# A layer with 64 experts on one core: another order of the experts, eight early loads on ScalarE's queue, and a last pass written out tile by tile

## The chip, the core and the metric

The kernel runs on one core of a Trainium2 chip. The metric is the device time of one execution in microseconds (us). The core has five engines that each take their instructions in a fixed order: TensorE (PE, matrix products and transposes; PEld is its weight loads), VectorE (DVE), ScalarE (ACT), GpSimd (POOL) and SyncE (SP, which here issues most transfers). Sixteen DMA engines move data between HBM and the core's SBUF. The instructions of one engine never overtake each other; a wait at its head holds all that is queued behind it.

## The reference

One layer for 1024 tokens of width 1024: first token mixers (differential attention beside a state space scan), then a mixture of experts. The change lies in the second half:

```python
h = modulate(rmsnorm(x, g_pre_ffn[li]), sh2, sc2)
f_lat = moe_ffn(h.reshape(-1, d), *moe_w)          # 64 experts, 8 for each token, and one shared
x = x + gt2 * rmsnorm(f_lat.reshape(x.shape), g_post_ffn[li])

def expert_block(args):
    tok_b, w_b, e = args
    xb = h[tok_b]
    hid = jax.nn.silu(xb @ w_e_gate[e]) * (xb @ w_e_up[e])
    return (hid @ w_e_down[e]) * w_b[:, None].astype(h.dtype)
...
routed = jax.ops.segment_sum(out.reshape(n_pad, d), buf_tok, num_segments=n_tok)
return routed + shared
```

Everything is float32. The gate, up and down matrices of one expert are 1 MB each, so 192 MB of weights are read in this half, each matrix once.

## The kernel before

Attention, scan and output projection come first, up to about 1800 us; the change touches none of it. Then tokens are routed, and the shared expert runs on eight tiles of 128 tokens.

**Experts, blocks, places.** Experts are renumbered on the chip by their load, the fullest first, and each number has a fixed room for tokens (CAPS, line 37): 416, 384, 352, 320 for experts 0 to 3, 256 to 128 for 4 to 39, 112 for 40 to 48, 96 for 49 to 56, 80 for 57 to 59 and 64 for 60 to 63. A room is cut into blocks of at most 128 tokens, 98 in all: expert 0 has four, 1 to 3 three, experts up to 28 at least two ("heavy"), 29 to 63 one ("light"). Tokens that find no room would go through a leftover loop (`overflow`, L2330; its count is read from `novf` at L2336 and the loop at L2337 runs that many times, here none).

**Two kinds of blocks.** A block of more than 64 tokens works with weights that were split into a high and a low float32r part (`weights`, `weights_down`: ScalarE casts the high part, L164, VectorE subtracts, L171), with three products for each pair: 24 for gate and up, 12 for down, on 128x512. A block of at most 64 tokens (`whole_block`) reads the raw weights as they were loaded, packed two or four ways on PE; a block of 64 has 64 small gate and up products and 8 down products. Experts 60 to 63 have only such a block ("pure") and are not split. Experts 0, 3 and 13 to 28 have one besides larger blocks, and their raw buffers are given back only when both the split and the block have read them.

**Buffers and queues.** `loads` (L2000) puts three transfers for each expert on SP's queue (helper `dma`, L212): gate, up, down, in the order of the list `order`. There are 4 raw buffers for gate and up, 2 for down (`draw`), 4 high and 4 low tiles for gate and up (`gh`, `gl`), 2 and 2 for down (`dh`, `dl`): two experts' worth of each. Buffers of a ring are handed out in turn. POOL gathers each block's tokens (L262) and adds its result to one of two sums in HBM (`scatter_add`, L268), `yacc[1]` and `yacc[0]` alternately (`turn`, L1995).

**What sets the order.** `Flow` (L107 on) is a planner that runs while the kernel is built: every stage is a generator, and it writes each engine's instructions in the order in which its own clocks would let the stages go on. The list `order` (L2304 and L2305) is what it starts from: one heavy expert, one light one, and so on: 0, 29, 1, 30, 2, 31, 3, 32, and so on to 28, 57, then 58 to 63. I call the position in this list a place: expert 2 is at place 4, 4 at 8, 13 at 26, 20 at 40, 28 at 56 and 63 at 63.

**The last pass** (`final`, L2397): the two sums are loaded as 8 tiles y and 8 tiles z of 128x1024 on SP, in turn y0, z0, y1, z1 and so on, then x for the last two tiles (PLAIN, L31). A group of FG tiles (4, 2, 2) is added (L171), squared on ScalarE with its row sums (L156), a root is computed by 12 small steps on VectorE, and the tiles are scaled (L187). Six tiles are added to the output in HBM by accumulating transfers on POOL (`add_to`, L274), since the output already holds x; for the last two, x is added on VectorE, and a plain write goes out on SP. The planner sets the order of these steps:

```python
for t in range(8):
    for i in range(2):
        F.dma((y, z)[i][t], s.yacc[i][t * P:(t + 1) * P, :])
...
for n in FG:
    F.spawn(1, rows(t, n))
```

## Time and profile before

| what | us |
|---|---|
| median of three runs | 2785.7 (2785.47 to 2786.71) |
| profiled execution | 2800.41 |
| its span, first to last instruction | 2798.6 |
| PE busy | 2618.5 (94%) |
| VectorE busy | 2013.0 (72%) |
| ScalarE busy | 1340.7 (48%) |
| POOL busy | 903.0 (32%) |
| SP's transfers, share of 16 engines | 45.6% |
| POOL's transfers, share of 16 engines | 14.8% |

All times in the sections below are counted from the first instruction of the profiled execution. The mean granted clock of PE is 0.976 of full speed over the span. The chain that ended last, followed back from the last instruction, lies for 58% on PE, 10% on DMA and 9% on VectorE. Busy shares are means over stages of different kinds; the routed experts take from about 1830 to 2740, the last pass the rest.

### The profile page before, as it was taken

The numbers are of one execution on the slowest core, as the hardware profiler recorded it, in microseconds if no ns is written. First come the engines' busy times: TensorE is split into PE (matmuls) and PEld (weight loads), VectorE is DVE, ScalarE is ACT, GpSimd is POOL, SyncE is SP. The second block draws the span as 40 slices with busy tenths as digits, with TensorE's granted clock in tenths as the row PEclk, the third lists the DMA queues.
The fourth block names the chain that finished last, engine by engine and source line by source line (L and its number), as shares of the span: only waits on it lengthen the run. The fifth ranks groups of instructions, "written<-read, shape, count | busy, mean of one in ns | idle before, by whom it ended". The sixth has DMA issues, their size and how long they took to land.

```text
span 2798.6 us, 41131 instructions
## 1 busy us (share of the span) xinstructions
PE 2618.5 (94%) x14561; PEld 2101.1 (75%) x14561; DVE 2013.0 (72%) x4680; ACT 1340.7 (48%) x2104; POOL 903.0 (32%) x669
## 2 busy tenths in 40 slices
PE   7999999999999999999999999889999999999991
PEld 4888878778788777888887687668887776777660
DVE  6877133768686749888894767867788877788863
ACT  4211123344443546666664422435666656676651
POOL 0111010545353520000000000055656656677841
PEclk9999999999999999999999999999999999999996
DMA  7767253242334354223233953568899998999997
GB/s 277 224 206 216 64 143 105 67 139 91 121 91 132 106 172 145 82 91 141 93 102 125 292 179 133 188 216 264 276 309 297 315 299 278 307 321 328 314 316 233
DMA packets 275409, 545.67 MB, mean 195 GB/s; under 512 B 31562, under 2 KB 166835, under 8 KB 248194
## 3 DMA queue, kind: packets, MB, share of 16 engines
q1 hardware_dynamic: 239330, 437.14, 45.6%
q0 software_dynamic: 35872, 105.88, 14.8%
q8 instruction: 115, 1.88, 0.3%
q14 instruction: 92, 0.75, 0.1%
HBM read 433.78 MB, written 124.73 MB: 200 GB/s over the span
## 4 chain that ended last, share of the span: by engine, by line
PE 58%; DMA 10%; DVE 9%; issue 4%; ACT 2%; POOL 2%; SPq 0%; POOLq 0%; ACTq 0%; DVEq 0%
PE gu L148 16%; PE acc L148 10%; PE dn L148 9%; PE bacc L148 5%; PE sps L148 5%; PE pv L148 4%; DMA cr<-cumd,crow 3%; PE xt L152 2%; PE tr L152 2%; PE aux L148 2%; DVE G L187 2%; DMA qk<-qk 2%; DMA braw<-in_w_branch_attn_dram 1%; DVE gl L171 1%; DVE W L180 1%
## 5 line engine op out<-in xcount | busy, mean ns | idle before, releaser
L171 DVE TENSOR_TENSOR gl<-raw,gh 128x1024 fp32r<-128x1024 f32 x240 | 288.2, 1218 | 35.4 <-ACT gh L164 33.7
L148 PE MATMUL acc<-hh,hi 128*128 128x512 f32 (+2 forms) x760 | 304.7, 401 | 1.3 <-DVE ux L187 1.3
L148 PE MATMUL acc<-hl,hi 128*128 128x512 f32 (+2 forms) x760 | 289.3, 381 | 0.0
L164 ACT CAST gh<-raw 128x1024 fp32r<-128x1024 f32 x240 | 246.6, 1050 | 88.0 <-PE gu L148 59.2
L148 PE MATMUL acc<-hh,lo 128*128 128x512 f32 (+1 forms) x736 | 280.9, 382 | 2.5 <-DVE lo L171 2.5
L148 PE MATMUL gu<-gh,xh 128*128 128x512 f32 (+3 forms) x672 | 278.4, 414 | 0.6 <-ACT gh L164 0.6
L148 PE MATMUL gu<-gl,xh 128*128 128x512 f32 (+3 forms) x672 | 264.5, 394 | 6.2 <-DVE gl L171 4.4
L148 PE MATMUL gu<-gh,xl 128*128 128x512 f32 (+3 forms) x672 | 264.5, 394 | 0.0
L193 DVE TENSOR_SCALAR_CACHE_REDUCE e<-sps 128x512 f32<-128x512 f32 (+1 forms) x384 | 214.4, 597 | 32.9 <-PE sps L148 32.6
L262 POOL DMA_INDIRECT cr<-cumd,crow x98 | 123.4, 1260 | 316.1 <-DMA wtab<-sc 281.2
L268 POOL DMA_INDIRECT yacc<-y,tk x98 | 181.3, 1850 | 96.8 <-issue 23.2
L148 PE MATMUL sps<-qk 128*128 128x512 f32 (+1 forms) x768 | 195.6, 386 | 9.3 <-DMA qk<-qk 5.1
L156 ACT ACTIVATE e<-e,st 128x1280 f32<-128x1280 f32 x128 | 174.7, 1366 | 32.0 <-DVE st L202 31.8
L262 POOL DMA_INDIRECT wc<-wtab,tk x98 | 148.6, 1516 | 121.0 <-DVE tk L182 85.9
L148 PE MATMUL acc<-hi,hh 128*128 128x512 f32 x448 | 181.3, 405 | 0.0
L148 PE MATMUL acc<-hi,hl 128*128 128x512 f32 x448 | 176.2, 393 | 0.4 <-DVE hl L171 0.4
L148 PE MATMUL acc<-lo,hh 128*128 128x512 f32 x448 | 176.0, 393 | 0.0
L148 PEld LDWEIGHTS sps<-qk 128*128 128x128 f32 x768 | 141.2, 192 | 41.3 <-DVE e L193 8.3
L148 PEld LDWEIGHTS acc<-hh,hi 128*128 128x128 f32 (+1 forms) x760 | 142.6, 188 | 32.9 <-issue 4.0
L148 PE MATMUL pv<-wr,vv 128*128 128x256 f32 x640 | 165.1, 381 | 0.0
L148 PEld LDWEIGHTS acc<-hl,hi 128*128 128x128 f32 (+1 forms) x760 | 142.6, 188 | 27.4 <-issue 0.8
L148 PEld LDWEIGHTS acc<-hh,lo 128*128 128x128 f32 x736 | 138.7, 188 | 32.1 <-DVE lo L171 3.3
(327 smaller groups left out, 6264.3 us busy)
## 6 DMA issues: line engine op xcount, KB each, us to landing
raw<-in_w_e_gate_dram SPq DMA_DIRECT2D x64, 1024.0 KB
raw<-in_w_e_up_dram SPq DMA_DIRECT2D x64, 1024.0 KB
draw<-in_w_e_down_dram SPq DMA_DIRECT2D x64, 1024.0 KB
qk<-qk POOLq DMA_DIRECT2D x16, 1664.0 KB
raw<-in_w_in_dram SPq DMA_DIRECT2D x40, 512.0 KB
wada<-in_w_ada_dram SPq DMA_DIRECT2D x32, 512.0 KB
R<-acd SPq DMA_DIRECT2D x64, 256.0 KB
qk<-sa SPq DMA_DIRECT2D x52, 256.0 KB
```

The lines of the kernel that those rows point to most:

```text
L148: s.nc.tensor.matmul(out, l, r, start=start, stop=stop)
L152: s.nc.tensor.transpose(out, in_, ident)
L156: s.nc.scalar.activation(out, in_, fn, **kw)
L164: s.nc.scalar.copy(out, in_)
L171: s.nc.vector.tensor_tensor(out, a, b, op=op)
L180: s.nc.vector.tensor_scalar(out, a, s1, s2, op0=op0)
L187: s.nc.vector.scalar_tensor_tensor(out, a, sc, b, op0=op0, op1=op1)
L193: s.nc.vector.tensor_scalar(out, a, s1, None, op0=op0, op1=op1, accum_out=acc)
L262: s.nc.gpsimd.indirect_dma_start(out=out, out_offset=None, in_=table, in_offset=bass.IndirectOffsetOnAxis(ap=idx, axis=0), **kw)
L268: s.nc.gpsimd.indirect_dma_start(out=table, out_offset=bass.IndirectOffsetOnAxis(ap=idx, axis=0), in_=in_, in_offset=None, compute_op=ALU. ...
```

## The change

It has three parts. The list `order` comes from a new function, `balanced`: it prices an expert's work on PE (9.3, 7.2 or 4.4 for a block by its kind) and its load (8.6 + 0.03 for each token of room), and takes an expert with more work than load, then one with less, so that the running difference stays near zero; the last three light ones are kept for the end. The eight z tiles get a pool of their own after the experts and before the leftover loop, and are loaded on ScalarE's queue instead of SP's. The last pass is written in the order of the string TAIL (a: add and square, r: roots of a group, s: scale and write) with groups of 3, 3 and 2 tiles.

```diff
--- before.py
+++ after.py
@@ -28,7 +28,8 @@
 ND, NR, NDR, NA = 2, 4, 2, 5
 LEAD = 2
 SLACK = 400.0, 0.0, 200.0, 0.0, 800.0, 400.0, 1500.0
-FG = 4, 2, 2
+FG = 3, 3, 2
+TAIL = "a0 a1 a2 a3 r0 s0 a4 s1 a5 s2 a6 r1 s3 a7 s4 s5 r2 s6 s7"
 PLAIN = 2
 HELD = 6, 1, 1
 RP = 0
@@ -2301,8 +2302,7 @@
             whole = {r: [] for r in blocks if any(ways(q[2]) > 1 for q in blocks[r])}
             pure = {r for r in whole if len(blocks[r]) == 1}
             uses = {}
-            many, one = [r for r in range(64) if len(blocks[r]) > 1], [r for r in range(64) if len(blocks[r]) == 1]
-            order = [q for i in range(max(len(many), len(one))) for q in many[i:i + 1] + one[i:i + 1]]
+            order = s.balanced(blocks)
             arena = Arena(*(q.get() for q in (gls, ghs, ghs, gls)))
             F.spawn(0, loads())
             F.spawn(2, weights())
@@ -2326,6 +2326,26 @@
             F.spawn(1, routed())
             F.run()
             s.close("em", "ew", "eps")
+            fz = s.open("fz")
+            s.z = [fz.tile([P, D], F32, name=f"z{t}") for t in range(8)]
+            for t in range(8):
+                F.dma(s.z[t], s.yacc[1][t * P:(t + 1) * P, :], eng=nc.scalar)
+
+    def balanced(s, blocks):
+
+        pe = {r: sum({1: 9.3, 2: 7.2, 4: 4.4}[ways(q[2])] for q in b) for r, b in blocks.items()}
+        ld = {r: 8.6 + 0.03 * CAPS[r] for r in blocks}
+        k = sum(pe.values()) / sum(ld.values())
+        last = [r for r in sorted(blocks) if len(blocks[r]) == 1][-3:]
+        left, out, d = [r for r in sorted(blocks) if r not in last], [], 0.0
+        more = {r: pe[r] - k * ld[r] for r in left}
+        while left:
+            same = [q for q in left if (more[q] > 0) == (d <= 0)] or left
+            r = max(same, key=lambda q: abs(more[q]))
+            left.remove(r)
+            out.append(r)
+            d += more[r]
+        return out + last
 
     def overflow(s):
 
@@ -2397,45 +2417,42 @@
     def final(s):
         F = s.F
         with s.pool("fin") as fp:
-            y, z, x1 = ([fp.tile([P, D], F32, name=f"{n}{t}") for t in range(8)] for n in ("y", "z", "x1"))
+            y, x1 = ([fp.tile([P, D], F32, name=f"{n}{t}") for t in range(8)] for n in ("y", "x1"))
+            z = s.z
             for t in range(8):
-                for i in range(2):
-                    F.dma((y, z)[i][t], s.yacc[i][t * P:(t + 1) * P, :])
+                F.dma(y[t], s.yacc[0][t * P:(t + 1) * P, :])
             for t in range(8 - PLAIN, 8):
                 F.dma(x1[t], s.out[0][t * P:(t + 1) * P, :])
             sqs = s.ring(fp, [P, D], "sq", 2)
-
-            def rows(t0, n):
-
-                ss = fp.tile([P, n], F32, name=f"nss{t0}")
-                for i in range(n):
-                    q = y[t0 + i]
-                    yield [q, z[t0 + i], "DVE"]
-                    F.tt(q, q, z[t0 + i], ALU.add)
-                    yield [q, sqs, "ACT"]
-                    sq = sqs.get()
-                    F.act(sq, q, AF.Square, accum_out=ss[:, i:i + 1])
-                    sqs.put(sq)
-                yield [ss, "DVE"]
-                F.ts(ss, ss, 1.0 / D, EPS, ALU.mult, ALU.add)
-                r = yield from s.rsqrt(fp, ss, n, f"z{t0}")
-                for i in range(n):
-                    q, o = y[t0 + i], s.out[0][(t0 + i) * P:(t0 + i + 1) * P, :]
-                    yield [r, "DVE"]
-                    F.stt(q, q, r[:, i:i + 1], s.gpost, ALU.mult, ALU.mult)
-                    if t0 + i >= 8 - PLAIN:
-                        F.tt(q, q, x1[t0 + i], ALU.add)
-                        F.dma(o, q)
-                        continue
-                    yield [q, "POOL"]
+            ss = [fp.tile([P, n], F32, name=f"nss{g}") for g, n in enumerate(FG)]
+            at = [(g, i) for g, n in enumerate(FG) for i in range(n)]
+            root = {}
+
+            def add(t):
+                g, i = at[t]
+                F.tt(y[t], y[t], z[t], ALU.add)
+                sq = sqs.get()
+                F.act(sq, y[t], AF.Square, accum_out=ss[g][:, i:i + 1])
+                sqs.put(sq)
+
+            def roots(g):
+                F.ts(ss[g], ss[g], 1.0 / D, EPS, ALU.mult, ALU.add)
+                root[g] = s.drain(s.rsqrt(fp, ss[g], FG[g], f"z{g}"))
+
+            def scale(t):
+                g, i = at[t]
+                q, o = y[t], s.out[0][t * P:(t + 1) * P, :]
+                F.stt(q, q, root[g][:, i:i + 1], s.gpost, ALU.mult, ALU.mult)
+                if t >= 8 - PLAIN:
+                    F.tt(q, q, x1[t], ALU.add)
+                    F.dma(o, q)
+                else:
                     F.add_to(o, q)
 
-            t = 0
-            for n in FG:
-                F.spawn(1, rows(t, n))
-                t += n
+            for q in TAIL.split():
+                {"a": add, "r": roots, "s": scale}[q[0]](int(q[1]))
             F.run()
-        s.close("rw")
+        s.close("fz", "rw")
 
     def run(s):
         tc, nc, F = s.tc, s.nc, s.F
```

With these prices the list is, with a bar where the pattern changes: 0, 60, 29, 30 | 31, 2, 32, 33, 34, 1, 35, 36, 37, 3, 38, 39, 40, 11, 41, 42, 12, 43, 9, 44, 45, 10, 46, 8, 47, 4, 48, 5, 49, 6, 50, 51, 7, 52 | 13, 53, 14, 54, 15, 55, 56, 16, 57, 17, 58, 18, 59 | 19, 20, 21, 22, 23, 24, 25, 26, 27, 28 | 61, 62, 63. Lines of the changed kernel are one higher than before up to `order`, and 20 higher from `overflow` on.

The order shows on POOL where the first routed blocks are gathered (xg: a block's tokens, wc: their weights, cr: the table from which token numbers are made; tk: token numbers). Before, the blocks behind expert 0's are those of experts 29 and 1, all of 128 tokens:

```order
L262 DMA xg<-htab,tk 128x1024
L262 DMA wc<-wtab,tk 128x1
L262 DMA cr<-cumd,crow 128x128
L262 DMA wc<-wtab,tk 128x1
L262 DMA xg<-htab,tk 128x1024 x2
L262 DMA wc<-wtab,tk 128x1
L268 DMA yacc_13428<-y,tk 4096x256
```

Now the piece at the same place has the block of 64 tokens of expert 60, and the table read of a block of 96:

```order
L263 DMA xg<-htab,tk 64x1024
L263 DMA wc<-wtab,tk 128x1
L263 DMA cr<-cumd,crow 96x128
L263 DMA wc<-wtab,tk 128x1
L263 DMA xg<-htab,tk 128x1024
L269 DMA yacc_13428<-y,tk 4096x256
L263 DMA xg<-htab,tk 128x1024
```

The first scatter, of expert 0's block of 32, stands one step earlier, and a gather of 64 rows has come ahead of it.

On ScalarE at the end of the experts (novf: the count of tokens left over; dn: a block's down result), before:

```order
L156 ACTIVATE y_26499<-dn_26494,wc_25685 128x512
L2336 TENSOR_LOAD novf_16399
L2337 COMPARE_AND_BRANCH
L2337 UNCONDITIONAL_BRANCH x2
L2480 BRANCH_PREFETCH_HINT
```

Now:

```order
L157 ACTIVATE y_26499<-dn_26491,wc_25803 128x512
L213 DMA z0_26510<-yacc1_13428 128x1024
L213 DMA z1_26511<-yacc1_13428 128x1024
L2356 TENSOR_LOAD novf_16303
L2357 COMPARE_AND_BRANCH
```

and behind the loop's end:

```order
L2357 COMPARE_AND_BRANCH
L2357 UNCONDITIONAL_BRANCH
L213 DMA z2_26512<-yacc1_13428 128x1024
L213 DMA z3_26513<-yacc1_13428 128x1024
L213 DMA z4_26514<-yacc1_13428 128x1024
L213 DMA z5_26515<-yacc1_13428 128x1024
L213 DMA z6_26516<-yacc1_13428 128x1024
L213 DMA z7_26517<-yacc1_13428 128x1024
L157 ACTIVATE sq_26736,nss0_26732<-y0_26706 128x1024
```

Two of the eight z loads stand ahead of the leftover loop and six behind its end, ahead of the first square.

On VectorE in the last pass (rs_y: the roots of a group; raw: the gain; nss: sums of squares), before, from the first addition:

```order
L171 TENSOR_TENSOR y0_26687<-y0_26687,z0_26695 128x1024
L171 TENSOR_TENSOR y4_26691<-y4_26691,z4_26699 128x1024
L171 TENSOR_TENSOR y1_26688<-y1_26688,z1_26696 128x1024
L171 TENSOR_TENSOR y5_26692<-y5_26692,z5_26700 128x1024
L171 TENSOR_TENSOR y2_26689<-y2_26689,z2_26697 128x1024
L171 TENSOR_TENSOR y6_26693<-y6_26693,z6_26701 128x1024
L171 TENSOR_TENSOR y3_26690<-y3_26690,z3_26698 128x1024
L182 TENSOR_SCALAR nss4_26730<-nss4_26730 128x2
L171 TENSOR_TENSOR y7_26694<-y7_26694,z7_26702 128x1024
```

Now, behind the first four additions and the roots of group 0:

```order
L188 SCALAR_TENSOR_TENSOR y0_26706<-y0_26706,rs_y_26748,raw_26413 128x1024
L172 TENSOR_TENSOR y4_26710<-y4_26710,z4_26514 128x1024
L188 SCALAR_TENSOR_TENSOR y1_26707<-y1_26707,rs_y_26748,raw_26413 128x1024
L172 TENSOR_TENSOR y5_26711<-y5_26711,z5_26515 128x1024
L188 SCALAR_TENSOR_TENSOR y2_26708<-y2_26708,rs_y_26748,raw_26413 128x1024
L172 TENSOR_TENSOR y6_26712<-y6_26712,z6_26516 128x1024
L183 TENSOR_SCALAR nss1_26733<-nss1_26733 128x3
```

Before, seven additions stand ahead of the first step of a root, and the scalings come after all eight; now scalings of tiles 0 to 2 alternate with additions of tiles 4 to 6.

## Rows read from the trace of the kernel before

**Rows 1.** The page, busy time, share of the span and instructions of each engine.

```profile
PE 2618.5 (94%) x14561; PEld 2101.1 (75%) x14561; DVE 2013.0 (72%) x4680; ACT 1340.7 (48%) x2104; POOL 903.0 (32%) x669
```

**Rows 2.** Windows of the routed stage: length, busy time (count), granted clock, DMA share, GB/s.

```profile
1875.00:2050.00 175.00, 175.00 (x912) 143.62 (x911) 134.75 (x243) 103.34 (x157) 101.65 (x74) 1.00 0.83 256
2050.00:2100.00 50.00, 48.83 (x241) 40.53 (x240) 42.31 (x73) 32.68 (x47) 30.14 (x20) 1.00 0.97 330
2100.00:2275.00 175.00, 172.55 (x896) 135.52 (x895) 148.69 (x261) 111.32 (x167) 112.77 (x76) 0.99 0.95 305
2275.00:2425.00 150.00, 140.47 (x902) 103.79 (x902) 112.48 (x198) 92.76 (x142) 95.78 (x63) 0.98 0.93 293
2425.00:2550.00 125.00, 124.01 (x900) 92.00 (x897) 108.59 (x197) 86.83 (x135) 90.55 (x59) 1.00 1.00 320
2550.00:2725.00 175.00, 163.12 (x1208) 116.15 (x1208) 135.25 (x229) 106.77 (x174) 115.39 (x69) 0.98 0.96 317
```

**Rows 3.** Waits of SP's queue, 1850 to 2735: us in total, times, longest.

```profile
SPq L212 <- DVE dl L171: 326.2, 47, 18.8
SPq L212 <- DVE gl L171: 264.7, 69, 17.6
```

**Rows 4.** Timeline of SP: gate loads of places 4, 8, 26, 40, 56, 63.

```profile
1890.59 0.33 SPq L212 DMA_DIRECT2D raw<-in_w_e_gate_dram  x1
...
1969.93 0.33 SPq L212 DMA_DIRECT2D raw<-in_w_e_gate_dram  x1
...
2226.91 0.33 SPq L212 DMA_DIRECT2D raw<-in_w_e_gate_dram  x1
...
2434.66 0.33 SPq L212 DMA_DIRECT2D raw<-in_w_e_gate_dram  x1
...
2643.02 0.33 SPq L212 DMA_DIRECT2D raw<-in_w_e_gate_dram  x1
...
2720.33 0.33 SPq L212 DMA_DIRECT2D raw<-in_w_e_gate_dram  x1
```

**Rows 5.** Windows of the last pass, columns as in rows 2.

```profile
2746.00:2769.00 23.00, 0.00 (x0) 0.00 (x0) 9.07 (x9) 7.66 (x13) 0.00 (x0) 0.50 1.01 401
2769.00:2774.00 5.00, 0.00 (x0) 0.00 (x0) 5.00 (x32) 1.52 (x4) 0.67 (x1) 0.50 0.09 36
2774.00:2794.00 20.00, 0.00 (x0) 0.00 (x0) 10.69 (x15) 0.00 (x0) 4.62 (x6) 0.50 0.99 209
```

**Rows 6.** Timeline of the end, all engines, 2738 to 2799.

```profile
2740.35 1.55 POOL L268 DMA_INDIRECT yacc<-y,tk  x1 [5.41 <-ACTq L2337]
2744.89 0.32 SPq L212 DMA_DIRECT2D y<-yacc  x1
...
2749.66 1.22 DVE L171 TENSOR_TENSOR y<-y,z 128x1024 f32<-128x1024 f32 x1 [12.99 <-DMA z<-yacc]
...
2773.33 0.96 POOL L274 DMA_DIRECT2D out_dram<-y  x1 [31.43 <-DVE rs_y L187]
...
2782.44 2.80 SPq L212 DMA_DIRECT2D out_dram<-y  x2
2783.64 1.22 DVE L171 TENSOR_TENSOR y<-y,x 128x1024 f32<-128x1024 f32 x1
```

**Rows 7.** Timeline of PE: expert 0's last product, product pitch, blocks of 64 tokens.

```profile
1885.10 0.39 PE L148 MATMUL dn<-dh,hl 128*128 128x512 f32 x1
...
2272.12 0.39 PE L148 MATMUL gu<-gh,xl 128*128 128x512 f32 x1
2272.35 0.40 PE L148 MATMUL gu<-gh,xh 128*128 128x512 f32 x1
...
2718.29 3.81 PE L148 MATMUL gu<-raw,xh 128*64 128x128 f32 x64
...
2725.26 3.80 PE L148 MATMUL gu<-raw,xh 128*64 128x128 f32 x64
```

**Rows 8.** Groups by form, 2742 to 2800: busy us, mean ns, idle before, releaser.

```profile
L187 DVE SCALAR_TENSOR_TENSOR y<-y,rs_y,raw 128x1024 f32<-128x1024 f32 x8 | 10.1, 1279 | 0.0
L171 DVE TENSOR_TENSOR y<-y,z 128x1024 f32<-128x1024 f32 x8 | 9.5, 1222 | 23.3 <-DMA z<-yacc 23.0
```

## The prediction

> **What bounds the kernel now.** I read the page first, then tables by stage, then SyncE's queue, then the end in order of time. On the page [rows 1] TensorE (PE) is busy 94% of the span: only what makes PE wait, or what comes after PE has stopped, can be saved. The change starts at the routed experts. By stage [rows 2] PE is busy 175.00 of 175 us at 1875 to 2050, where the DMA engines are busy only 0.83. From 2050 on it is the other way round: the DMA share is 0.93 to 1.00, and PE loses 2.45, 9.53, 0.99 and 11.88 us in the windows of 2100, 2275, 2425 and 2550, with 1.17 at 2050 together 26.0. So the heavy experts wait for PE while transfers idle, and the light ones wait for transfers. SyncE's queue (SP) shows how loads are held [rows 3]: 326.2 us until a down buffer has been split (dl), 264.7 until a gate or up buffer has (gl); loads run only two experts ahead of PE.
>
> I date progress by the issue of an expert's gate load [rows 4]. Between 1890.59 (place 4 of the old order) and 2720.33 (the last) lie 829.7 us. Behind PE's end comes the last pass, where PE does nothing: the DMA engines are full (1.01, 401 GB/s) at 2746 to 2769, all but idle (0.09) at 2769 to 2774, full again (0.99 at 209 GB/s) until 2794 [rows 5]. There the write-back sets the end.
>
> **Part 1, the order.** Nothing is computed more or less; instructions move on every engine, and SP's loads with them. PE's price of a block: 24 gate/up and 12 down products at 0.23 from start to start (2272.12 to 2272.35), 8.3, and some 1.0 of transposes, 9.3; a block of 64 tokens repeats every 6.97 (2718.29 to 2725.26), for which I keep the change's own 7.2; for one of 32, its 4.4 [rows 7].
>
> Old stretches against that price [rows 4]: places 8 to 26, nine pairs, 257.0 us for 251.1 of PE, a factor of 1.024; 26 to 40, seven pairs, 207.8 for 180.6, 1.15, or 14.8 per expert; 40 to 56, eight pairs, 208.4 for 186.8, 1.116, or 13.0 per expert with DMA full; 56 to 63 (one of 13.7, three of 9.3, three of 7.2), 77.3 for 63.2, 1.22, or 11.0 each.
>
> New start. Expert 60 comes second. Its raw buffers are read by PE itself, and the ring hands buffers out in turn, so expert 30's down load waits until PE has done 60. Expert 0's products end at 1885.5 [rows 7], 60 takes 7 more, and the gate of 31 goes out at about 1893. Early loads save nothing: PE is busy 1875 to 2050 without them.
> - From 31 to 52 (34 experts, PE 453.6): this mixes heavy with light so that PE need and transfers keep step; factor 1.024 as in places 8 to 26: 465.
> - 13, 53 to 18, 59 (13 experts, PE 164.1): the same mix as in places 26 to 40, between 13.0 and 14.8 per expert. I take the middle, 14.1: 184.
> - 19 to 28, ten in a row (PE 142.6): no light between them, so PE has 14.3 of work for each load, above the 13.0 that a load needed. If the lights of places 40 to 56 cost 1.22 of their 74.4, 90.8, the others took 117.6 for 112.4, a factor of 1.05: 150.
> - 61 and 62 at 11.0: 22.
>
> 1893 + 465 + 184 + 150 + 22 = 2714, against 2720.3: **-6**. What follows the last gate is the same (three blocks of 64). Bounds: below, all 26.0 us of PE's waits go, -26. Above, the ten at the lights' 1.22, 174 for 150: +18. I stand nearer the middle since the nearest rows (1.024, 14.8, 13.0) are the old mix's own.
>
> **Part 2, the loads of the second sum.** What the built order shows: only two of the eight (z0, z1) stand on ScalarE ahead of the leftover loop, six behind it. z0 and z1 need the 97th scatter; they can go at about 2740.2, beside the last scatter (2740.35), where the DMA engines are nearly idle. No ScalarE work is queued behind them but the loop. But every engine's way out of the loop now waits for their landing also, SP's y loads with it. Price from both sides: the first pair of before was added at 2749.66, 4.8 after its issue at 2744.89 [rows 6]; 4.8 from 2740.2 is 2745.0, and what lies between landing and the next issue is at most 3.0 (scatter's end 2741.9 to 2744.89). Delay 0.1 to 3.1; I take 1.0, since the lag after the landing is only a part of those 3.0. The Trainium skill (DMA: Bandwidth & Descriptors, section Anatomy of one DMA) gives a transfer 2.0 us and its bytes at 436 GB/s. By that estimate the pair lands at 2744.6, the last scatter (262 KB) at 2743.0, the delay is 1.6, and the sum is 0.6 worse; the trace of before shows no such pair by itself. What is gained: 1.05 MB is moved early, 2.6 us at 401 GB/s [rows 5]. The 16 transfers left, 524 KB or 1.31 us each, end at 2746.9 + 20.9 = 2768, 1 us before the old 2769. Two queues can't move more: the engines were already full.
>
> **Part 3, the last pass.** Before, VectorE added all eight pairs, then computed the roots, and issued the first write at 2773.33, six of them accumulating; the last two (plain) were issued from 2782.44, behind a backlog [rows 6]. Those 20.0 us at 0.99 are 19.8 us of transfer; less two plain writes at 1.31, 2.9 for each of six.
> After: the fourth add needs y3 and z3, some eight transfers after 2746.9, and ends near 2759.7. Behind it VectorE still has 4 adds at 1.22, 8 scales at 1.28 [rows 8], 2 additions of x at 1.22, and 3 chains of 12 small steps at 0.19 each (2.3): 4.9 + 10.2 + 2.4 + 6.9 = 24.4, to 2784.1. Before it ended at 2783.64 + 1.22 = 2784.9: **VectorE's end does not move.** But the writes start near 2763.5 in place of 2773.3, the first ones beside loads, and the backlog is drained by 2784. The last plain write, issued at about 2784.5, has moved its bytes by 2787.5, against 2794: **-6**. If the squares on ScalarE or late tiles stall VectorE by 4, -2; if the third chain hides, -8. The x loads of the last two tiles stay behind y on SP; they are needed 20 us later and cost nothing.
>
> **Sum:** -6 - 6 = -12 on the profiled execution (2800.41, span 2798.6), 2788.4. The median of the runs, 2785.7, lies 14.7 below it; I take the difference over: **2773.7**.
>
> **Rivals.** What can be told from no change here is about 0.2%, 5.6 us.
> 1. *Both engines stay full.* For: DMA was idle 29.75 us in the window of 1875 alone (0.17 of 175), room to bring the loads forward, and PE's waits are 26.0. Then -26 - 6 = -32, 2753.7. Against: only two experts' buffers lie between the two. 0.18.
> 2. *The order moves the waits.* DMA runs at 0.93 to 1.00 for 675 us [rows 2]; if the first 34 experts are held by transfers, a factor of 1.04 in place of 1.024, 7 us are lost there and 1893 to 2721 is the old time. Net -5, about 2780. In this case the result is within 0.2%. 0.22.
> 3. *Slower: ten in a row.* Experts 19 to 28 each have a block that reads raw weights, so their raw buffers are held until PE has done it and the split beside it; before, each was followed by a light one that holds none. If a load then comes as late as in the run of lights, a factor of 1.22, stretch 3 takes 174: +18 - 6 = +12, 2797.7. It decides from 167.6 us on (150 + 12 + 5.6), 16.8 per expert. For: 1.22 was measured where experts of one kind followed each other. Against: those had 9 us of PE per load, these 14.3. 0.15.
> 4. *The change doesn't do what it says.* Of eight loads two go early; if also the delay is 3.1 and the tail gives nothing, only the order is left: -6, 2779.7. 0.03.
>
> **Numbers.** My forecast 0.42, with -20 to -6 as its own range. Faster: 0.42, 0.18 and a part of the fourth, 0.62. Same 0.22, slower 0.16 (the third, and the rest of the fourth, should the order bring nothing either). The range reaches from rival 1 to rival 3, 2752 to 2797; what it leaves out is a gain above 26 or a loss in several stretches at once.
>
> **What would show it.** Right: the gate of 31 near 1893; PE's busy share over 0.97 after 2275; 28's gate about 15 us after 27's; z0 and z1 issued before the loop's end, y0 at 2745.9 less the routed gain; a first write some 10 us earlier against VectorE's end, and no DMA backlog of over 4 us behind VectorE's last instruction. Wrong: PE idle in the ten, DMA under 0.9 there (rival 3); DMA at 1.00 with PE waiting before the 52nd (rival 2); VectorE waiting for z2 to z7 (the six late loads).

## The result, and the profile after

| | before | changed |
|---|---|---|
| median of six runs, us | 2786.12 (2778.98 to 2787.56) | 2757.4 (2749.47 to 2762.38) |
| profiled execution, us | 2800.41 | 2762.38 |
| its span | 2798.6 | 2760.1 |
| last scatter of the routed experts | 2740.35 | 2709.74 |
| from there to the end | 58.25 | 50.36 |

The ratio is 0.9899, with a 95% interval of 0.9881 to 0.9917: about 29 us are gone, where 12 were forecast. The time lies inside the range and close to rival 1 (2753.7), not to the forecast (2773.7).

The page of the changed kernel, its row of busy times (it answers to [rows 1]):

```profile
PE 2610.2 (95%) x14561; PEld 2099.0 (76%) x14561; DVE 2012.4 (73%) x4680; ACT 1341.9 (49%) x2104; POOL 920.9 (33%) x669
```

The same windows of the routed stage as in [rows 2], columns as there (the last one ends at 2700, since the stage ends earlier):

```profile
2050.00:2100.00 50.00, 49.68 (x245) 40.48 (x245) 42.41 (x75) 34.87 (x50) 38.10 (x23) 1.00 0.95 296
2100.00:2275.00 175.00, 174.25 (x866) 135.57 (x865) 156.12 (x268) 117.52 (x172) 124.09 (x76) 1.00 1.00 334
2275.00:2425.00 150.00, 147.43 (x841) 113.45 (x841) 126.36 (x222) 97.75 (x147) 100.74 (x66) 1.00 0.98 315
2425.00:2550.00 125.00, 124.82 (x835) 90.92 (x833) 107.07 (x194) 86.15 (x133) 90.61 (x57) 1.00 0.95 310
2550.00:2700.00 150.00, 149.14 (x1394) 111.39 (x1395) 104.93 (x196) 87.68 (x155) 101.93 (x69) 1.00 0.96 302
```

PE's lost time in these windows is 0.32, 0.75, 2.57, 0.18 and 0.86 us, where [rows 2] had 1.17, 2.45, 9.53, 0.99 and 11.88. The column of the granted clock says a second thing: 1.00 throughout, where [rows 2] had 0.98 to 0.99 in three of the windows. That second thing is what the prediction left out; what it is worth is worked out under "What a wait costs". PE is busy 8.3 us less over the whole execution (2618.5 to 2610.2) for the same instructions, but 4.6 of these lie in the packed products of the blocks of 32 tokens (22.9 to 18.3 us), which go by the chip (last section).

The timeline of the end, all engines (it answers to [rows 6]):

```profile
2706.86 1.55 POOL L269 DMA_INDIRECT yacc<-y,tk  x1 [3.60 <-ACT hh L165]
...
2709.74 1.55 POOL L269 DMA_INDIRECT yacc<-y,tk  x1 [1.33 <-ACT y L157]
...
2711.29 0.82 ACTq L213 DMA_DIRECT2D z<-yacc  x2
...
2717.34 0.33 SPq L213 DMA_DIRECT2D y<-yacc  x1
...
2735.04 0.96 POOL L275 DMA_DIRECT2D out_dram<-y  x1 [23.75 <-DMA z<-yacc]
...
2752.49 2.80 SPq L213 DMA_DIRECT2D out_dram<-y  x2
...
2753.70 1.22 DVE L172 TENSOR_TENSOR y<-y,x 128x1024 f32<-128x1024 f32 x1
```

The first write starts 25.30 us after the last scatter (before 32.98), and from VectorE's last instruction to the end only 5.2 us are left (2754.92 to 2760.1; before 13.7). But y0 is issued 7.60 us after the last scatter, where it was 4.54: the two early z loads hold up the way out of the leftover loop.

The windows of the last pass (as [rows 5]) show the gap in the middle closed; the DMA engines are full in all three windows, from the loads into the writes:

```profile
2717.00:2739.00 22.00, 0.00 (x0) 0.00 (x0) 12.31 (x21) 6.34 (x11) 1.83 (x2) 0.50 0.96 374
2739.00:2745.00 6.00, 0.00 (x0) 0.00 (x0) 5.58 (x16) 1.60 (x4) 1.44 (x2) 0.50 1.07 221
2745.00:2757.00 12.00, 0.00 (x0) 0.00 (x0) 9.43 (x19) 1.15 (x2) 1.98 (x3) 0.50 1.05 228
```

**Two profiles are not enough here.** The groups of runs below were made on several chips, and the kernel before took 2798.9, 2784.2, 2795.3 and 2788.3 us on them. So times are compared as ratios within a group, and stages only between profiles from one chip.

### The profile page after: what moved, and what is told of

Read it like the earlier page. It is cut to its first block, busy times and chain, and to the rows that moved or that the text cites. A ratio compares the mean times of both kernels' runs of the same rounds, so it can differ in the third digit from the quotient of the medians.

```text
span 2760.1 us, 41127 instructions
## 1 busy us (share of the span) xinstructions
PE 2610.2 (95%) x14561; PEld 2099.0 (76%) x14561; DVE 2012.4 (73%) x4680; ACT 1341.9 (49%) x2104; POOL 920.9 (33%) x669
## 4 chain that ended last, share of the span: by engine, by line
PE 63%; DMA 8%; DVE 8%; issue 3%; POOL 2%; ACT 2%; SPq 0%; ACTq 0%; POOLq 0%; DVEq 0%
PE gu L149 18%; PE acc L149 11%; PE dn L149 9%; PE bacc L149 6%; PE sps L149 5%; PE pv L149 4%; PE xt L153 3%; DMA cr<-cumd,crow 2%; PE tr L153 2%; PE aux L149 2%; DVE G L188 2%; DMA qk<-qk 2%; PE py L149 1%; DVE W L181 1%; PE hT L153 1%
## 5 line engine op out<-in xcount | busy, mean ns | idle before, releaser
L263 POOL DMA_INDIRECT cr<-cumd,crow x98 | 134.1, 1368 | 319.0 <-DMA wtab<-sc 282.5
L269 POOL DMA_INDIRECT yacc<-y,tk x98 | 189.4, 1933 | 80.8 <-DMA yacc<-y,tk 14.4
```

The costliest lines, as they stand in the source:

```text
L263: s.nc.gpsimd.indirect_dma_start(out=out, out_offset=None, in_=table, in_offset=bass.IndirectOffsetOnAxis(ap=idx, axis=0), **kw)
L269: s.nc.gpsimd.indirect_dma_start(out=table, out_offset=bass.IndirectOffsetOnAxis(ap=idx, axis=0), in_=in_, in_offset=None, compute_op=ALU. ...
```

## The experiments

The first two profiles, of before and of the changed kernel, I call the first profiles. The theory after the result (A): the old order makes PE wait, every wait also costs clock behind it, and the balanced order takes most of both away; the last pass gives its 6 to 8 us on top. The rivals are named with each run.

### The kernel before, again, and each part by itself

The kernel before, unchanged:

> The kernel before, unchanged, for a second profile. Theory A (the old order makes PE wait, and PE's clock falls behind the waits): the routed stage again shows 20 to 35 us of PE idle time between 1850 and 2740 and windows of 10 us with a granted clock under 0.95, whatever the span. Rival C (the profile of before was taken in a long execution, 14.7 us over the median of the runs, and the 38 us between the two profiles are partly that): the span is 2775 to 2788, and what is missing against 2798.6 lies in the routed stage (last scatter 5 to 15 us earlier than 2740.35), not in the last pass (58.2 from the last scatter to the end).

Measured: 2797.29 us, span 2795.5, last scatter at 2739.62, 55.88 us from there to the end. The theory's waits are there (34.1 us of PE idle time, below). Rival C is not decided by this run: on this chip the kernel before takes 2798.9 us in the median, so a long profile is the usual thing here. It is right in part: 11 of the 38 us between the first profiles have to do with the chip (last section).

The order alone:

```diff
-            many, one = [...], [...]
-            order = [q for i in range(max(len(many), len(one))) for q in many[i:i + 1] + one[i:i + 1]]
+            order = s.balanced(blocks)
```

> Only the balanced order; the sums are loaded and the last pass is done as before. Theory A: about 2766, 20 us (0.7%) under before, with PE idle of 15 us or less in the routed stage and hardly a window of 10 us under a granted clock of 0.95; from the last scatter to the end 58 us as before. Rival B (the last pass brings most of the 28 us): 2778 or more.

Measured: 2775.95 us (2773.87 to 2782.76), the kernel before 2798.94 on this chip, ratio 0.9917 (0.9902 to 0.9932), 23 us or 0.83%, where theory A had 0.7%; rival B is out. Last scatter at 2717.79, 21.8 us earlier than in the run before; from there 56.21 us, as without the change.

The old order with the early z loads and the last pass:

```diff
-            order = s.balanced(blocks)
+            many, one = [...], [...]
+            order = [q for i in range(max(len(many), len(one))) for q in many[i:i + 1] + one[i:i + 1]]
```

> The old order with the early z loads and the last pass in the order of TAIL. Theory A: the last pass brings 8 us and nothing in the routed stage, about 2778; from the last scatter to the end 50 to 51 us in place of 58.2, its first write 25 us after the last scatter in place of 33. Rival B: 2766 or less. Rival D (without the new order the early z loads collide with the last experts): 2784 or more.

Measured: 2791.27 us (2787.92 to 2797.89), ratio 0.997 (0.9958 to 0.9981), 7.7 us. Last scatter at 2741.18, as before; first write 23.13 us behind it, end 48.42 us behind it. So the order brings three quarters and the last pass one quarter, each by itself: 23.0 and 7.7. Together they bring less than their sum: 26.9 us on this chip (2772.05 us for the changed kernel, in the section on the early z loads), and on top of the new order the early loads and the last pass bring only 3.9.

The windows of one stage in two profiles of that chip, first the kernel before again, then the order alone (columns as in [rows 2]):

```profile
1859.00:2050.00 191.00, 189.57 (x981) 155.48 (x980) 146.58 (x263) 113.15 (x172) 110.62 (x79) 1.00 0.83 263
2050.00:2300.00 250.00, 243.61 (x1289) 191.85 (x1287) 207.58 (x362) 158.96 (x237) 157.12 (x106) 0.99 0.95 308
2300.00:2420.00 120.00, 111.17 (x711) 82.60 (x712) 89.56 (x158) 71.88 (x110) 78.83 (x50) 0.97 0.91 283
2420.00:2640.00 220.00, 210.77 (x1573) 155.13 (x1572) 186.97 (x338) 148.75 (x234) 164.84 (x103) 1.00 0.99 322
2640.00:2739.00 99.00, 90.83 (x706) 63.16 (x704) 60.38 (x100) 51.98 (x90) 46.81 (x28) 1.00 0.94 307
```

```profile
1859.00:2050.00 191.00, 185.74 (x997) 149.57 (x996) 150.82 (x260) 119.08 (x178) 111.42 (x76) 0.99 0.90 297
2050.00:2300.00 250.00, 248.91 (x1232) 196.34 (x1231) 220.11 (x380) 167.56 (x244) 176.00 (x109) 1.00 0.99 325
2300.00:2420.00 120.00, 118.37 (x682) 90.36 (x680) 102.96 (x181) 79.56 (x120) 84.47 (x54) 1.00 0.98 316
2420.00:2640.00 220.00, 216.29 (x1657) 157.11 (x1656) 180.47 (x332) 146.28 (x233) 160.06 (x106) 1.00 0.94 304
2640.00:2717.00 77.00, 74.79 (x692) 54.45 (x690) 35.00 (x66) 31.88 (x64) 32.58 (x24) 1.00 0.85 253
```

PE's idle time falls from 34.1 us (1.4, 6.4, 8.8, 9.2, 8.2) to 13.9 (5.3, 1.1, 1.6, 3.7, 2.2). The transfers have moved ahead: the DMA share of the first window rises from 0.83 to 0.90, that of the last falls from 0.94 to 0.85. The new order pays 3.9 us more waiting at the start for 24 less behind it.

### What a wait costs

The idle time alone explains 20.1 of the 21.8 us. Something is left, and the clock gives a part of it. The timeline of PE in the first profile of the kernel before, at the longest wait of the routed stage:

```profile
2371.19 0.40 PE L148 MATMUL dn<-dl,hh 128*128 128x512 f32 x1
2375.35 0.80 PE L148 MATMUL dn<-dh,hl 128*128 128x512 f32 x1 [3.77 <-DVE hl L171]
2375.94 0.63 PE L148 MATMUL dn<-dh,hh 128*128 128x512 f32 x1
2376.37 0.63 PE L148 MATMUL dn<-dl,hh 128*128 128x512 f32 x1
...
2380.42 0.63 PE L148 MATMUL gu<-gl,xh 128*112 128x512 f32 x1
...
2381.19 0.39 PE L148 MATMUL gu<-gh,xh 128*112 128x512 f32 x1
2381.42 0.39 PE L148 MATMUL gu<-gl,xh 128*112 128x512 f32 x1
```

The window in between, columns as in [rows 2]:

```profile
2377.00:2380.00 3.00, 3.00 (x9) 2.25 (x9) 0.62 (x1) 0.69 (x1) 2.49 (x2) 0.50 0.92 169
```

PE waits 3.77 us. Behind that, products start every 0.43 us (2375.94 to 2376.37) until about 2380.9, and then every 0.23 again: the granted clock is 0.50, the lower of the clock's two levels (1.2 GHz for 2.4), for some 5 us. This time counts as busy. About twelve products at 0.2 us more are 2.4 us on top of the 3.8. The Trainium skill (TensorE: Matmul & The Clock Gate, section HAM oscillation — how this bites in real kernels) describes the same, work that starts at the lower clock again after a wait for data; the trace agrees.

What PE waits for here is not a load of weights. It is the low part of the hidden values (hl), and VectorE is late with it. VectorE's timeline ahead of the wait:

```profile
2367.36 0.06 DVE L287 MEMSET wc<- 112x1 f32 x1
2370.26 0.26 DVE L180 TENSOR_SCALAR cr<-cr,srel 128x128 bf16<-128x128 bf16 x1 [2.80 <-DMA cr<-cumd,crow]
...
2374.88 0.42 DVE L171 TENSOR_TENSOR hl<-hT,hh 128x256 fp32r<-128x256 f32 x1
```

VectorE stands 2.80 us idle until a gather of a token table (cr) has landed, while the DMA engines are full (share 1.03 at 2368 to 2371), and then works off what is queued behind it; hl comes last. In the second profile of before it is the same wait: VectorE idle for 3.00 us, PE for 4.83. Over the stage VectorE stands 39 to 50 us on these gathers in the old order and the three other unbalanced lists below, and 17 to 25 in the eight profiles of balanced ones. So the transfers reach PE through VectorE's queue, at least here; no run changes these gathers alone, so their share in the gain is not shown.

Taken over the routed stage in windows of 10 us, from about 1860 to the last scatter, with the clock's loss as the length times what is missing to a granted clock of 1 (some of it falls into idle time, so the sum counts a little twice):

| kernel | last scatter | PE idle | clock's loss | sum |
|---|---|---|---|---|
| before again | 2739.6 | 34.0 | 5.1 | 39.1 |
| old order, new last pass | 2741.2 | 29.1 | 8.6 | 37.7 |
| new order alone | 2717.8 | 13.9 | 1.7 | 15.6 |
| new order, new last pass, next run | 2718.0 | 13.7 | 3.4 | 17.1 |

All four are from one chip. From the old order to the new, with the old last pass, the sum falls by 23.5 and the last scatter comes 21.8 earlier; with the new last pass it is 20.6 and 23.2. So the sum agrees with the last scatter to 2.6 us; the idle time alone gives 20.1 and 15.4. The clock's loss of one order differs from profile to profile: 5.1 to 8.6 us in three profiles of the old, 0 to 3.4 in seven of the new.

### Where the early z loads stand

The z loads written behind the loop in the code, their tiles left where they are:

```diff
-            for t in range(8):
-                F.dma(s.z[t], s.yacc[1][t * P:(t + 1) * P, :], eng=nc.scalar)
...
             z = s.z
+            for t in range(8):
+                F.dma(z[t], s.yacc[1][t * P:(t + 1) * P, :], eng=s.nc.scalar)
```

> The changed kernel with all eight z loads behind the leftover loop, on ScalarE's queue still. If the early loads cost as much as they bring (theory A: y0 was issued 7.6 us after the last scatter in place of 4.5, against 2.6 us of transfer moved ahead): y0 goes 4.5 us after the last scatter, the loads end within 1 us of the changed kernel's, and the end comes 50 to 51 us after the last scatter; the time is that of the changed kernel within 0.2%. If the early loads bring their 2.6 us (rival E): 53 us. If they only delay (rival F): 47 to 48 us.

This edit moved nothing: in the built program z0 and z1 stood ahead of the loop as before, so the run is the changed kernel a second time, on the chip of the three runs above. It took 2772.05 us (2767.71 to 2772.91), ratio 0.9895 (0.988 to 0.9911); y0 came 8.71 us after the last scatter, the end 52.31.

So the z tiles were put into the last pass's own pool, which is opened behind the loop:

```diff
-            fz = s.open("fz")
-            s.z = [...]
...
-            y, x1 = (... for n in ("y", "x1"))
+            y, z, x1 = (... for n in ("y", "z", "x1"))
...
-                F.dma(y[t], s.yacc[0][t * P:(t + 1) * P, :])
+                for i in range(2):
+                    F.dma((y, z)[i][t], s.yacc[i][t * P:(t + 1) * P, :])
```

> The balanced order and the last pass by TAIL, but all eight z tiles loaded behind the leftover loop, in turn with y on SyncE's queue, so that the loop's end waits for the last scatter alone. (In the run before, the z loads were written behind the loop but two of them still stood ahead of it, since their tiles lay in a pool opened ahead of it; here the tiles lie in the last pass's own pool.) If the early loads delay more than they bring (theory F): y0 4.5 us after the last scatter in place of 7.6 to 8.7, the first write at 22 to 23.5 in place of 25.3 to 26.6, the end at 47 to 49.5 in place of 50.4 to 52.3; the ratio 0.988 or less. If they bring as much as they cost (theory A): the end at 50 to 52. If they bring their 2.6 us (rival E): 53.

Measured: 2754.6 us (2754.14 to 2755.72), ratio 0.9892 (0.9878 to 0.9906). The timeline of its end:

```profile
2703.87 1.55 POOL L269 DMA_INDIRECT yacc<-y,tk  x1 [1.33 <-ACTq L2353]
2708.36 0.32 SPq L213 DMA_DIRECT2D y<-yacc  x1
...
2726.06 0.96 POOL L275 DMA_DIRECT2D out_dram<-y  x1 [20.63 <-DMA z<-yacc]
```

y0 is back at 4.49, the first write at 22.19, and the span of 2752.5 ends 48.63 us after the last scatter, all as theory F had it; the ratio is not the 0.988 or less that it named. But this edit changes two things, the place of the z loads and their queue.

The same with z on ScalarE's queue, behind the loop (`eng=s.nc.scalar`):

> As the run before it, but z on ScalarE's queue, behind the loop. If the second queue brings nothing of its own (the DMA engines are full with one): first write and end within 1 us of the run before, counted from the last scatter. If two queues fill the engines sooner (rival): the first write 1.5 us or more earlier.

Measured: 2755.50 us; y0 4.36, first write 24.64, end 50.94 us after the last scatter. In this one execution the second queue does not help: the end is 2.3 us later than with the single one, which brings y and z in pairs, and the first write 2.5. Neither expectation had that. This run also parts the two things: with all z loads behind the loop, on the queue that the changed kernel uses, the end is at 50.94, where the changed kernel has 50.36 to 52.31. So what the run before gained lies with the queue, not with the place, as far as one execution shows it.

Both once more on one chip:

> The changed kernel once more, on the chip of the next run. Its ratio to before again 0.9875 to 0.9915; from the last scatter to the end 50 to 52.5 us. If the chip runs the four-way packed products of a block of 32 in 2.0 us each (17.6 us for the nine in all), before is at 2784 to 2787; if it needs 28 us or more for them, at 2795 to 2800.

Measured: 2753.99 us (2751.23 to 2755.74), ratio 0.9888 (0.9869 to 0.9907); end 51.08 us after the last scatter. The packed products take 2.0 us for a block, and before is at 2788.28, 1.3 us over what was expected with that.

> The balanced order with z behind the leftover loop on SyncE's queue, on the same chip as the run before it. Theory F (the early loads delay the loop's end by more than they bring): 2 to 4 us (0.07 to 0.15%) under the changed kernel, with 48 to 49.5 us from the last scatter to the end. Theory A (no difference): within 1 us of it.

Measured: 2758.12 us (2748.98 to 2760.49), ratio 0.9898 (0.988 to 0.9916); end 48.59 us after the last scatter. In the stage this version is 2.5 us ahead, as theory F says (51.08 and 48.59, and 50.36 to 52.31 against 48.63 on other chips), but after the run on ScalarE's queue that can't be put down to the early loads. In whole executions it is not seen: the median is 4.1 us longer, where theory F had 2 to 4 less, and each kernel's own runs lie 4 to 12 us apart. Whether this version beats the changed kernel stays open.

### What of the order counts

The old alternation with only the end changed (four of the last lights moved forward; early z loads and the new last pass kept):

```diff
-            order = s.balanced(blocks)
+            early, one, last = one[28:32], one[:28], one[32:]
+            order = [q for i in range(29) for q in many[i:i + 1] + (early[i // 8:i // 8 + 1] if i % 8 == 0 else []) + one[i:i + 1]] + last
```

> The changed kernel with the old alternation of one heavy and one light expert, in which only four of the last lights (57 to 60) are moved forward, one to every eighth pair, so that three lights are left for the end as in the balanced order. Rival T (the run of lights at the end was what the order gained): ratio 0.988 to 0.991, as the changed kernel. Theory A (the imbalance of the whole stage, heavy first and light later, makes PE wait in the second half): PE idle time falls only by the 6 us of the end, from 34 to 25 to 30 us, and the ratio is 0.994 to 0.996 (6 us of order and 8 of the last pass).

Measured: 2776.21 us (2768.98 to 2782.06), ratio 0.9966 (0.9953 to 0.9978); PE idle 27.2 us, clock's loss 10.2. The last pass's share (0.997) explains all of it; rival T is out, and so is theory A's ratio: the 6 us of the end did not show. The idle time behind 2640 did fall, to 3.6 us, and the clock's loss is above that of the old order (10.2 for 5.1 to 8.6). That the one came back as the other is likely but not shown, since the profiles are from different chips.

Another sequence with the same balance:

```diff
-            r = max(same, key=lambda q: abs(more[q]))
+            r = min(same, key=lambda q: abs(more[q]))
```

> The changed kernel with another sequence that keeps the same running difference near zero: of the experts of the wanted sign the one with the smallest difference is taken, not the largest, so it begins with 21, 57, 22, 23, 24 and ends with 2, 38, 39, 60, 0, 61, 62, 63. Theory A (the balance is what counts): PE idle time of 10 to 20 us and a ratio of 0.989 to 0.992. Rival H (a long expert ahead, so that the first loads have time, and small steps at the end count as much): PE waits over 10 us before 1950, and the ratio is 0.995 or more.

Measured: 2761.8 us (2760.49 to 2767.27), ratio 0.9925 (0.9912 to 0.9937); PE idle 11.6 us, clock's loss 5.1. Idle time as theory A says, the ratio just beside its range: a quite different list keeps most of the gain. PE waits 4.7 us before 1950, not the 10 of rival H. Against the run with z behind the loop, on the same chip, its last scatter is 3.4 us later (2707.27 and 2703.87); the sums of idle time and clock's loss differ by 4.2.

The balance in coarser steps:

```diff
+        up = True
...
-            same = [q for q in left if (more[q] > 0) == (d <= 0)] or left
+            up = d <= -10 or (up and d < 10)
+            same = [q for q in left if (more[q] > 0) == up] or left
```

> The changed kernel with a balanced order of coarser steps: experts of one sign are taken until the running difference of work and load (in the change's own prices) passes 10 us, then those of the other sign until it passes -10; so up to nine light ones follow each other, and up to ten heavy ones. In the old order the difference stands at 24 to 30 from the 7th to the 40th place, in the balanced one at -2.4 to 4 after the first three places. Theory A (the two experts of buffers bridge only short runs): PE idle time of 20 to 40 us, the ratio 0.993 to 0.997. Rival G (only the share of heavy and light over the whole stage counts, short swings are bridged): PE idle time of 10 to 16 us and 0.9885 to 0.991, as the changed kernel.

Measured: 2824.1 us (2820.42 to 2829.13), ratio 1.0103 (1.0085 to 1.0121): slower than the kernel before, worse than either theory had it. PE idle 45.1 us, clock's loss 20.4. Two windows of it, one in the run of nine lights, 36 to 44, one in that of ten, 45 to 54:

```profile
2050.00:2150.00 100.00, 88.20 (x410) 68.12 (x410) 83.52 (x135) 66.10 (x93) 72.98 (x38) 0.97 0.95 307
...
2250.00:2350.00 100.00, 92.86 (x445) 72.35 (x444) 78.95 (x144) 61.48 (x90) 59.59 (x40) 0.97 0.84 253
```

Runs of lights leave PE 7 to 12 us short in 100, and the clock goes with it. The expectation had reckoned with the idle time, not with the clock.

All heavy ones first, then all lights (`order = sorted(blocks)`):

> The changed kernel with the experts in the order of their numbers: all heavy ones, then all light ones, the largest imbalance that there is (88 us in the change's prices). Theory A: PE is busy without waits up to about 2400 while the DMA engines idle, then 32 light experts go at the speed of their loads, 12 to 13 us each for 9.3 of work: PE idle time of 80 to 120 us with PE's granted clock under 1 in most of that stretch, and the execution 60 to 120 us over the changed kernel's, slower than the kernel before. Rival G': loads of light experts alone run faster (11.0 us each, as in the last seven places of the old order): 30 to 60 us over the changed kernel's.

Measured, in one execution: 2854.72 us; the kernel before 2795.3 on that chip. PE idle 66.3 us, clock's loss 27.2. Against the changed kernel, which by its ratio of 0.99 would be at about 2767 there, it is some 87 us slower: inside theory A's 60 to 120, with less idle time than it said. The lights go at 12.0 us each by their gates (34 from 2376 to 2784), as theory A says, not at 11.0. Two windows of them:

```profile
2400.00:2500.00 100.00, 89.05 (x403) 69.28 (x402) 87.08 (x138) 67.66 (x93) 57.32 (x39) 0.97 1.02 355
...
2600.00:2700.00 100.00, 85.53 (x378) 59.41 (x376) 84.69 (x139) 65.21 (x94) 76.51 (x38) 0.93 0.96 317
```

## Why the prediction was right and wrong

**What bounds the kernel: right in the main.** Transfers idle under the heavy experts, PE waits under the light ones. The runs put a price on it: the old order and three other unbalanced lists gave 27 to 66 us of PE's idle time, the two balanced lists 7 to 14. That the light ones wait for transfers is right less directly than it was said: in the second profile of before, 23 of PE's 34.1 us were ended by VectorE, 11.5 of them by hl, and only 1.5 by a split weight (gl).

**The order, -6 forecast, -22 to -23 measured: wrong in size.** The step that failed is the sum of the stretches in part 1. Its prices (1.024, 14.1 for each expert, 1.05) were read from the old mix and carry that mix's waits with them, though the new order is there to remove these: -6 leaves 20 of the 26.0 us of PE's waits standing, and the run with the order alone left 13.9 of 34.1. Gates in the run with the order alone, SyncE's timeline (experts 31, 13, 19, 61 and 63; the second row is 31's down load):

```profile
1881.18 0.33 SPq L212 DMA_DIRECT2D raw<-in_w_e_gate_dram  x1
...
1890.23 0.33 SPq L212 DMA_DIRECT2D draw<-in_w_e_down_dram  x1
...
2346.42 0.33 SPq L212 DMA_DIRECT2D raw<-in_w_e_gate_dram  x1
...
2517.48 0.33 SPq L212 DMA_DIRECT2D raw<-in_w_e_gate_dram  x1
...
2663.75 0.33 SPq L212 DMA_DIRECT2D raw<-in_w_e_gate_dram  x1
...
2692.60 0.33 SPq L212 DMA_DIRECT2D raw<-in_w_e_gate_dram  x1
```

| term | forecast | measured |
|---|---|---|
| gate of 31 | 1893 | 1881.2 |
| 31 to 13, 34 experts | 465 | 465.2 |
| 13 to 19, 13 experts | 184 | 171.1 |
| 19 to 61, the ten | 150 | 146.3 |
| 61 to 63 | 22 | 28.9 |
| last gate to last scatter | 20 | 25.2 |
| last scatter | 2734 | 2717.8 |

- *The start.* It was said that expert 30's down load waits until PE has done 60. The buffer it took was free earlier; it was 31's down load that waited for 60 (1890.23, behind 60's down products at 1888.25). The gate of 31 went out 12 us early. PE gained nothing by it: up to 2050 it waits 3.9 us more than before.
- *The 13 experts.* 14.1 us each were taken as the middle between 13.0 and 14.8; the middle is 13.9, or 181 in all. Measured 13.2. The nearer row was the one with full DMA engines: the 14.8 of places 26 to 40 held PE's waits in it, which were the very thing to be removed.
- *The ten in a row.* 150 forecast, 146.3 here and 137.4 in the first profile of the changed kernel. The 8.9 us between these two are about what the packed products of these experts take longer on the first chip (22.1 for 14.2, pauses included). Rival 3 would have needed 167.6. It fails: with 14.3 us of work for each load PE waits 4.8 us in the ten, and 0.8 in the changed kernel's profile.
- *The end.* 12 us longer, since loads now run ahead of PE there; the gates then no longer date PE's work. The early start and the late end cancel (-12 and +12); what is left is the 13 and the ten, -17. A sum by PE's own waits would not have had these two errors.
- *The bound.* -26 was called the most that there is, all of PE's waits. It held, but it was too small for what could be gained: a wait costs its idle time and the clock behind it, 34.0 and 5.1 us in the kernel before on that chip, of which 23.5 are gone. The [rows 2] had the second part in their clock column (0.99, 0.98, 0.98); the prediction put it at nothing. With 3.4 of the 23.5 it is the smaller part of the miss.

Rival 1 was what happened on the whole, though not by filling the DMA engines to the last (their share is 0.85 to 0.99): PE idles 14 us instead of 34. Rival 2 is refuted for the first 34 experts, which took the forecast 465.

**The early z loads, a delay of 1.0 forecast.** With the old order it is 0.94 (y0 5.48 after the last scatter, before 4.54). With the new one 3.1 to 4.2 (7.60 to 8.71). What failed is the time at which they can start: the last two scatters are now 2.88 us apart (2706.86 and 2709.74; before 6.96), so z0 must wait for the 97th until 1.55 us after the last one was issued, where -0.2 was forecast. The estimate of 1.6 by the Trainium skill's figure for a transfer (DMA: Bandwidth & Descriptors, section Anatomy of one DMA) missed for the same cause. That figure is given there for transfers that GpSimd issues; the z loads are ScalarE's. In the changed kernel's other two profiles SyncE waits 4.2 and 3.8 us in all at the loop's end until z has landed. What the prediction did not price is the second queue: with z behind the loop, the end is 2.3 us later on it than with y and z in pairs on one (50.94 and 48.63), and the early loads bring about as much as they delay (50.36 to 52.31 against 50.94).

**The last pass, -6 forecast: right.** -7.7 us with the old order, in the stage 55.88 to 48.42; 56.21 to 52.31, -3.9, with the new one on the same chip, where the delay takes its part. VectorE's end against the last scatter moved by 0.7 us in the changed kernel (44.51 to 45.18), as said not at all; the first write came 7.7 us earlier against the last scatter, and the writes that are left behind VectorE's end take 3 us in place of 9.

**The signs named ahead.** PE's share behind 2275 was to be over 0.97: 0.98, 1.00, 0.99. 28's gate was to follow 27's by 15 us: 14.0 in the run with the order alone, 11.3 in the changed kernel. The gate of 31 was to be near 1893: 1880.5. The DMA share in the ten, under 0.9 by rival 3, is 0.91 in the run with the order alone and 0.95 in the changed kernel.

## What to carry to other kernels

Where loads are two steps ahead and no more, it pays to keep work and load in balance from step to step. The size of the running difference alone doesn't tell the cost, though. In the change's own prices it lies between -2.5 and 9.5 behind the first places in both balanced lists (the -2.4 to 4 of the coarse list's expectation hold for the changed kernel's list from the 15th to the 52nd place only), and PE idles 7 to 14 us. In the coarse list it lies between -12 and 13, with runs of nine and ten lights, and PE idles 45; in the old order it stands at 24 to 30 for long without such runs, and PE idles 29 to 34. So long runs of light experts cost more here than a steady lead of work. Price such a change by the waits of the engine that sets the end, and add to each wait what its clock loses behind it; don't date the work by the issue of loads, which may run ahead. A load that is moved ahead of a loop with a count read at run time becomes something that the way out of the loop waits for: here it cost 3.1 to 4.2 us, about what it brought.

## What had not been expected of the hardware

**Some chips stretch packed products.** A block of 32 tokens has 64 gate and up products, packed four ways on PE. In the run with the order alone (first fence) and in the changed kernel (second), the timeline of PE at expert 0's block:

```profile
1836.52 1.48 PE L148 MATMUL gu<-raw,xh 128*32 128x128 f32 x31
1839.12 0.32 PE L148 MATMUL gu<-raw,xh 128*32 128x128 f32 x2 [1.12 <-issue]
1840.56 0.29 PE L148 MATMUL gu<-raw,xh 128*32 128x128 f32 x1 [1.12 <-issue]
1841.98 0.39 PE L148 MATMUL gu<-raw,xh 128*32 128x128 f32 x2 [1.13 <-issue]
...
```

```profile
1844.58 2.03 PE L149 MATMUL gu<-raw,xh 128*32 128x128 f32 x64
```

The same instructions take 10.2 us with pauses of 1.1 us between a product or two, or 2.0 without a pause. It goes by the chip, not by the kernel: the changed kernel has both. Summed over the nine blocks of 32, pauses included, the six profiles from the two chips on which the kernel before took 2795 and 2799 us have 28.6 to 34.3 us, the seven from chips with 2784 to 2788 have 18.3 each. The 10 to 16 us more are of the size of the 7 to 15 us between those chips; that they are its cause is not shown. 11 of the 38 us between the first profiles are of this kind (29.3 before, 18.3 after). Why these chips pause there stays open.

**A wait is paid twice.** The lower clock behind PE's waits, 5 to 9 us in the old order and 27 in the worst one, stands in no row of waits, and most of it counts as busy time.
